# A hybrid decoder step on one core: the product of the squares' sum moved behind the third unit of the gated projection

## The chip, the core and the metric

One core of a Trainium2 chip runs the whole step as one program. The metric is the device time in microseconds of one execution; the time of a version is the median of its runs. The engines are TensorE (PE in the rows; its weight loads are PEld), VectorE (DVE), ScalarE (ACT), GpSimd (POOL) and SyncE (SP), which here issues most of the transfers.

## The reference

Two layers of a decoder run on 520 tokens (512 of a prompt and 8 new ones), with a width of 1024. Each layer normalizes its input, projects it once to 7424 columns, and feeds a convolution branch and an attention branch, which are gated, merged and added to the input. The parts that matter here:

```python
def rms_norm(x, g):
    xf = x.astype(jnp.float32)
    y = xf * lax.rsqrt(jnp.mean(xf * xf, axis=-1, keepdims=True) + EPS)
    return (y * g.astype(jnp.float32)).astype(x.dtype)

def hybrid_layer(x, ...):
    h = rms_norm(x, norm_g)
    z = jnp.einsum('ntd,dc->ntc', h, w_in)
    glu, gate_a, q, k, v, gate_b, mg_a, mg_b = split_in(z)
    u = glu[..., :CONV_WIDTH] * jax.nn.sigmoid(glu[..., CONV_WIDTH:])
    ...
    return x + jnp.einsum('ntd,de->nte', y, w_out), ...
```

## The kernel before, in words

**Layout.** Everything is held transposed: the width lies on the 128 partitions in 8 row tiles, and the 520 tokens on the free axis, in two halves of 260. All weights of a layer are cut into 82 blocks of 1024 x 128. One block is a `Unit` (line 101): it is loaded as `raw` (512 KB, line 123, by SP's queue), ScalarE casts it to a rounded `whi` (line 126), and VectorE makes the rest `wlo` (line 127). A row tile is likewise kept as a rounded part and a rest. `step(half, k)` (line 130) issues three matmuls: whi by the rounded row, wlo by the rounded row, whi by the row's rest. A half takes 8 steps, 24 matmuls, and a unit takes 48. There are two buffers of `raw` and three each of `whi` and `wlo`, so the load of a unit waits for the split (line 127) of the unit two before it, and its cast waits for the last matmul of the unit three before it.

**The start of a layer.** The gated projection takes 16 units, two for each of 8 column groups i: one for the sigmoid, one for the value. I number them from one: the first and second unit belong to i = 0, the third and fourth to i = 1, the fifth and sixth to i = 2, the seventh and eighth to i = 3, and the ninth begins i = 4. The first six units multiply the rows that are scaled by the norm's weight only (`xh`, `xl`), since the factor 1/rms is not known yet; it is multiplied in afterwards (lines 304 and 306). From the seventh on the units multiply the fully normed rows `hh` and their rests `hl`.

**The factor.** ScalarE squares the 8 row tiles (line 197), VectorE adds them up (line 165, seven additions to `ssum`). `totals` (line 175) multiplies the sum by a matrix of ones, one product for each half (line 170, in full float32; the trace shows each as two matmuls). `rstd` (line 178) takes the logarithm on ScalarE (L183), a scaled copy on VectorE (L184), the exponential on ScalarE (L186) and three more steps on VectorE (L187, L188, L189); its result is `R`. Then `normed` (line 263) makes the rows: L266 on VectorE multiplies by R, L97 on ScalarE casts, L98 on VectorE makes the rest. It is called for rows 0 to 2, 3 to 5 and 6 to 7, in the groups i = 0, 1 and 2. Its buffer `sq` has three places.

**The groups 0 to 2** copy the unit's results out of PSUM (lines 298 and 302, ScalarE), multiply by R (L304), take the sigmoid (L305), multiply by R again (L306) and by the value (L307). The result `u` goes to the convolution, which VectorE works off at low priority over the next hundreds of microseconds (L595).

**PSUM.** A unit's sums lie in one of two buffers `mm`. The third unit is `spare`: its halves lie in the tiles T and V instead, which are free at this stage, so that it can run before the first two units are copied out. A product of line 170 uses a tile S.

**What orders the work.** The text above does not fix the order on an engine. A planner runs through the program with its own idea of times and gives each engine, whenever it is free, the ready instruction that stands first in the text; the order that comes out is then fixed, and the engine keeps to it. `tc.issue_after(ins)` adds that what the block puts on the engine of `ins` is issued behind `ins`; it adds no wait for its end. `mark[1]` holds the last matmul issued (line 134). In the text of before, `R = rstd(sq.totals())` (line 286) stands behind the first two units and ahead of the third (line 289). In the first layer the first two units run as their rows arrive; in the second, they follow the previous layer's output.

Of the kernel before, what the change touches and what calls it, by code (L numbers as in the profile page):

```python
# [20 lines left out]
KT = 8  # L21
# [11 lines left out]
W_GLU, W_K, W_V, W_Q, W_GB, W_MB, W_MA, W_GA, W_YB, W_YA, W_OUT = (  # L33
    0, 16, 17, 18, 26, 34, 42, 50, 58, 66, 74)
# [10 lines left out]
def hybrid_step(ctx, tc, x_in, w_in, par, const, rope, conv_st, kc_in, vc_in,  # L45
# [17 lines left out]
    mark = [None, None, None]  # L63
# [5 lines left out]
    def g(dt=F32):  # L69
        return gp.tile([128, TOK], dt, tag="g", name=name("g"))  # L70
# [4 lines left out]
    def two(t):  # L75
        return t.rearrange("p (a b) -> p a b", a=2)
# [4 lines left out]
    def small(n):  # L81
        return sp.tile([128, n], F32, tag=f"sm{n}", name=name("sm"))

    def tmp(tag, bufs, n=TOK):
        return ap.tile([128, n], F32, tag=tag, bufs=bufs, name=name(tag))
# [9 lines left out]
    def split(src, n=TOK, new=g):  # L95
        hi, lo = new(F32R), new(F32R)
        A.copy(hi[:, :n], src)  # L97
        mark[0] = V.tensor_tensor(lo[:, :n], src, hi[:, :n].bitcast(F32), op=ALU.subtract)  # L98
        return hi, lo
# [78 lines left out]
    def rstd(sums, halves=(0, 1)):  # L178
        y0, v, a = tmp("y0", 1), tmp("v", 1), tmp("a", 1)
        c = slice(halves[0] * HALF, (halves[-1] + 1) * HALF)  # L180
        for hf, s in zip(halves, sums):
            h = slice(hf * HALF, (hf + 1) * HALF)
            A.activation(y0[:, h], s, AF.Ln, bias=eps, scale=1.0 / D)  # L183
            V.tensor_scalar(v[:, h], s, 1.0 / D, EPS, op0=ALU.mult, op1=ALU.add)  # L184
        y0, v, a = y0[:, c], v[:, c], a[:, c]
        A.activation(y0, y0, AF.Exp, scale=-0.5)  # L186
        V.scalar_tensor_tensor(a, y0, -0.5, y0, op0=ALU.mult, op1=ALU.mult)  # L187
        V.tensor_tensor(v, v, a, op=ALU.mult)  # L188
        V.scalar_tensor_tensor(v, v, 1.5, y0, op0=ALU.add, op1=ALU.mult)  # L189
        return v  # L190
# [33 lines left out]
    xs, xh, xl, sq = [], [], [], Sum()  # L224
# [28 lines left out]
    for l in range(L):  # L253
# [9 lines left out]
        def normed(lo, hi):  # L263
            for i in range(lo, hi):
                h = tmp("sq", 3)
                V.scalar_tensor_tensor(h, xs[i], pt[:, P_G + i:P_G + i + 1], R,  # L266
                                       op0=ALU.mult, op1=ALU.mult)
                a, b = split(h)
                hh.append(a)
                hl.append(b)  # L270
            return mark[0].ins

        EARLY = 3
        for i in range(KT):
            if i % 2 == 0:
                s = g()
                (nc.gpsimd if l else nc.sync).dma_start(s[:, :2 * NS * TAPS],
                                                        conv_st[l, :, i // 2, :])
                st.append(s[:, :2 * NS * TAPS].rearrange("p (i n k) -> p i n k", i=2, n=NS))
            src = (xh, xl) if i < EARLY else (hh, hl)  # L280
            if i == 0:
                for k in range(KT):
                    for u in first:
                        u.step(0, k)
                        u.step(1, k)
                R = rstd(sq.totals())
                a, b = first
            else:
                a = Unit(l, W_GLU + 2 * i, *src, spare=(i == 1))
                a.half(0)  # L290
                a.half(1)
            u = up.tile([128, PAD + TOK], F32, tag="u", name=f"u{l}_{i}")
            G.memset(u[:, :PAD], 0.0)
            uu = two(u[:, PAD:])
            sg = g()
            if i < EARLY:
                for hf in range(2):
                    A.copy(two(sg)[:, hf, :], a.acc[hf])
                if i > 0:
                    b = Unit(l, W_GLU + 2 * i + 1, *src)  # L300
                    b.both()
                A.copy(uu, b.ps)
                ready = normed((0, 3, 6)[i], (3, 6, 8)[i])
                V.tensor_tensor(sg, sg, R, op=ALU.mult)  # L304
                A.activation(sg, sg, AF.Sigmoid)  # L305
                V.tensor_tensor(sg, sg, R, op=ALU.mult)  # L306
                V.tensor_tensor(uu, uu, two(sg), op=ALU.mult)  # L307
            else:
                A.activation(two(sg), a.ps, AF.Sigmoid)
                z1 = Unit(l, W_GLU + 2 * i + 1, *src).both()  # L310
                V.tensor_tensor(uu, z1, two(sg), op=ALU.mult)
            V.tensor_copy(st[i // 2][:, i % 2, :, PAD:], u[:, PAD + T:].unsqueeze(2))
            nc.gpsimd.dma_start(ncp[l, :, i, :], u[:, T:T + PAD])
            us.append(u)
            if i % 2 == 1:
                nc.gpsimd.dma_start(ncs[l, :, i // 2, :],
                                    st[i // 2].rearrange("p i n k -> p (i n k)"))
                i0, pair = i - 1, (i - 1, i)
                n2 = 2 * NS * TAPS
                pr = tmp("sq", 3)[:, :n2]  # L320
                pr4 = pr.rearrange("p (i n k) -> p i n k", i=2, n=NS)
                wv = pt[:, P_CW + TAPS * i0:P_CW + TAPS * (i0 + 2)].rearrange("p (i k) -> p i k", i=2)
                for i in pair:
                    V.tensor_tensor(pr4[:, i - i0], st[i0 // 2][:, i - i0],
                                    wv[:, i - i0].unsqueeze(1).broadcast_to([128, NS, TAPS]),
                                    op=ALU.mult)
                sm = small(16)
                V.tensor_reduce(sm, pr.rearrange("p (m k) -> p m k", k=TAPS),
                                axis=mybir.AxisListType.X, op=ALU.add)
                for i in pair:  # L330
                    V.tensor_scalar(us[i][:, PAD + T:], sm[:, (i - i0) * NS:(i - i0 + 1) * NS],
                                    pt[:, P_CB + i:P_CB + i + 1], None, op0=ALU.add)
# [20 lines left out]
        for kv in range(2):  # L353
            a, b = g(F32R), g(F32R)
# [73 lines left out]
        for kv in range(2):  # L428
            src = qsam.rearrange("(t v) d n -> v d t n", v=2)[kv]
# [201 lines left out]
        for i in range(KT):  # L631
# [5 lines left out]
            a, b = split(e)  # L637
# [7 lines left out]
        for i in range(KT):  # L645
# [3 lines left out]
            a, b = split(mga[i], new=og)  # L649
# [14 lines left out]
        if not last:  # L664
            nres = dr.tile([128, KT, TOK], F32, tag="xres", bufs=1, name=f"xres{l}")
            pt = params(l + 1)
            xs, xh, xl, sq = [], [], [], Sum()
# [13 lines left out]
        sq = Sum()  # L681

        def finish(i, u, hf):
            x = two(xr[i])[:, hf, :]
            done = V.tensor_tensor(x, u.half(hf), x, op=ALU.add)  # L685
            s = tmp("sq", 3)
            A.activation(two(s)[:, hf, :], x, AF.Square)
            return sq.add(i, s, (hf,)) or done

        def scale(hf):  # L690
            return rstd([sq.total(hf)], (hf,))

        def store(hf, R, i0, i1):
            for i in range(i0, i1):
                x = two(xr[i])[:, hf, :]
                V.scalar_tensor_tensor(x, x, con[:, C_FG + i:C_FG + i + 1], R,  # L696
                                       op0=ALU.mult, op1=ALU.mult)
                (nc.sync if i % 2 else nc.scalar).dma_start(
                    y_out[:, i, hf * HALF:(hf + 1) * HALF], x)
# [10 lines left out]
        with tc.issue_after(mark[1].ins):  # L710
            R = scale(0)
            finish(5, units[0], 1)
# [117 lines left out]
```

## Time and profile before

| what | value |
|---|---|
| median of 3 runs | 1064.87 us |
| lowest and highest | 1064.74 and 1064.91 us |
| the profiled execution | 1064.98 us |
| its span, first to last instruction | 1063.2 us |
| mean granted clock of TensorE | 0.997 |
| instructions | 21526 |
| read from HBM, written to it | 107.66 MB, 17.36 MB |

The span is the time that the trace covers; the execution's own time has 1.78 us more around it. Times in rows are counted from the span's start. A row of the timeline gives the start, the time until the end of the last one, the engine, the line, the operation, the tile written and the tiles read, and how many instructions it merges. In brackets stands how long the engine was idle before it and what ended that.

### The profile page before, as it was taken

Reading aid. Unit: us, or ns where it says so; the run is one execution under the profiler, and the core shown is the slowest. Engines: PE = TensorE matmul, PEld = TensorE weight load, DVE = VectorE, ACT = ScalarE, POOL = GpSimd, SP = SyncE. Lnnn points to the kernel's source line nnn. Section 1 sums busy time; section 2 is a strip of 40 time slices with the busy share of each in tenths; the row PEclk is TensorE's granted clock in tenths of the full one; section 3 lists DMA queues with packets and bytes.
Section 4 is the critical chain, followed back from the end, with each engine's and each line's share of the span. In section 5 each row is a group of like instructions: output and inputs, shape, how many; then the busy total and the mean of one; then the engine's idle time right before and its main releaser. Section 6 shows DMA issues by size and latency. Waiting matters only on the chain.

```text
span 1063.2 us, 21526 instructions
## 1 busy us (share of the span) xinstructions
PE 1049.8 (99%) x8742; PEld 1034.9 (97%) x8742; DVE 855.4 (80%) x1572; ACT 516.5 (49%) x953; POOL 79.5 (7%) x180
## 2 busy tenths in 40 slices
PE   8999999999999999999999999999999999999996
PEld 8999999999999999999999999999999999999995
DVE  7999999999999587455569999899999976944545
ACT  7621433356667784224453234434576686822322
POOL 0001211001011000000101013100001000000000
PEclk9999999999999999999999999999999999999998
DMA  7334574332321215233334337633232212252312
GB/s 234 127 120 132 173 237 144 102 117 80 105 90 66 80 60 198 82 100 117 133 100 140 120 113 238 205 119 119 81 112 81 87 60 80 87 178 95 99 61 81
DMA packets 45220, 126.42 MB, mean 119 GB/s; under 512 B 6384, under 2 KB 10048, under 8 KB 45120
## 3 DMA queue, kind: packets, MB, share of 16 engines
q1 hardware_dynamic: 39024, 111.81, 32.0%
q0 software_dynamic: 4800, 12.16, 3.6%
q8 instruction: 68, 1.11, 0.4%
q10 hardware_dynamic: 1296, 1.07, 0.3%
q14 instruction: 32, 0.26, 0.1%
HBM read 107.66 MB, written 17.36 MB: 118 GB/s over the span
## 4 chain that ended last, share of the span: by engine, by line
PE 97%; DVE 1%; DMA 1%; SPq 0%; issue 0%; ACT 0%; DVEq 0%; ACTq 0%
PE mm L134 86%; PE S L506 3%; PE pv L541 3%; PE PT L532 2%; PE T L134 1%; PE S L170 1%; PE V L134 1%; DMA g<-x 1%; DMA raw<-w 0%; DVE g L696 0%; DVE ssum L165 0%; PE S L464 0%; PE pvs L486 0%; SPq L123 0%; PE S L348 0%
## 5 line engine op out<-in xcount | busy, mean ns | idle before, releaser
L134 PE MATMUL mm<-g,whi 128*128 128x260 f32 x4160 | 766.2, 284 | 1.0 <-ACT g L215 1.0
L134 PEld LDWEIGHTS mm<-g,whi 128*128 128x128 f32 x4160 | 644.8, 188 | 2.0 <-ACT g L215 1.2
L134 PE MATMUL mm<-g,wlo 128*128 128x260 f32 x2080 | 588.9, 283 | 0.0
L134 PEld LDWEIGHTS mm<-g,wlo 128*128 128x128 f32 x2080 | 392.0, 188 | 0.1
L595 DVE SCALAR_TENSOR_TENSOR acc<-u,par,acc 128x512 f32<-128x512 f32 x464 | 329.0, 744 | 0.2
L126 ACT CAST whi<-raw 128x1024 fp32r<-128x1024 f32 (+1 forms) x168 | 172.9, 1029 | 205.9 <-PE mm L134 165.1
L127 DVE TENSOR_TENSOR wlo<-raw,whi 128x1024 fp32r<-128x1024 f32 (+1 forms) x168 | 200.8, 1196 | 52.7 <-ACT whi L126 52.4
L134 PE MATMUL mm<-o,whi 128*128 128x260 f32 x992 | 179.3, 282 | 1.0 <-DVE g L685 1.0
L134 PEld LDWEIGHTS mm<-o,whi 128*128 128x128 f32 x992 | 153.1, 188 | 1.5 <-issue 0.8
L134 PE MATMUL mm<-o,wlo 128*128 128x260 f32 x496 | 139.5, 282 | 0.0
L134 PEld LDWEIGHTS mm<-o,wlo 128*128 128x128 f32 x496 | 93.2, 188 | 0.0
L518 ACT ACTIVATE p<-p,sm 128x257 f32<-128x257 f32 (+1 forms) x128 | 60.9, 479 | 18.7 <-DVE sm L512 18.6
L512 DVE CUSTOM_DVE_ANT_0 p<-S,con,nsk 128x256 f32<-128x256 f32 (+1 forms) x128 | 52.8, 447 | 7.9 <-PE PT L532 6.1
L534 ACT COPY pts<-PT 128x256 f32<-128x256 f32 (+1 forms) x64 | 33.7, 526 | 50.2 <-PE PT L532 50.2
L510 POOL COPY p<-nsk 128x2 f32<-128x2 f32 x64 | 26.0, 413 | 342.9 <-PE PT L532 289.0
L647 DVE TENSOR_TENSOR g<-mm,g 128x520 f32<-128x520 f32 x16 | 11.2, 700 | 43.1 <-PE mm L134 43.1
L506 PE MATMUL S<-g,g 128*128 128x256 f32 x256 | 41.6, 283 | 0.0
L445 ACT ACTIVATE g<-mm 128x520 f32<-128x520 f32 x16 | 9.7, 606 | 56.7 <-PE mm L134 56.7
L532 PE MATMUL PT<-con,p 128*128 128x128 f32 x224 | 35.6, 276 | 0.0
L506 PEld LDWEIGHTS S<-g,g 128*128 128x128 f32 x256 | 35.1, 188 | 0.0
L641 DVE TENSOR_TENSOR g<-mm,g 128x520 f32<-128x520 f32 x16 | 11.1, 695 | 28.8 <-PE mm L134 28.8
L522 ACT ACTIVATE p<-p,sm 128x128 f32<-128x128 f32 (+1 forms) x64 | 30.5, 480 | 7.5 <-DVE sm L521 7.3
(168 smaller groups left out, 817.5 us busy)
## 6 DMA issues: line engine op xcount, KB each, us to landing
raw<-w SPq DMA_DIRECT2D x162, 512.0 KB, 3.4
qscr<-g SPq DMA_DIRECT2D x32, 256.0 KB, 4.3
g<-qscr SPq DMA_DIRECT2D x32, 256.0 KB, 3.8
g<-x SPq DMA_DIRECT2D x16, 260.0 KB, 4.9
g<-rope POOLq DMA_DIRECT2D x8, 260.0 KB, 4.6
xres<-g POOLq DMA_DIRECT2D x8, 260.0 KB, 2.3
g<-xres SPq DMA_DIRECT2D x8, 260.0 KB, 4.9
ncs<-g POOLq DMA_DIRECT2D x8, 248.0 KB, 3.1
```

Source lines behind the costliest of these rows:

```text
L126: mark[2] = A.copy(self.hi[:, ks, :], self.raw[:, ks, :])
L127: mark[0] = V.tensor_tensor(self.lo[:, ks, :], self.raw[:, ks, :], self.hi[:, ks, :].bitcast(F32), op=ALU.subtract)
L134: mark[1] = PE.matmul(self.acc[hf], a[:, k, :], b[k][:, c], start=(k == 0 and j == 0), stop=(k == KT - 1 and j == 2))
L506: PE.matmul(S3[:, kv, :], qs[t, kv][:, b * 128:b * 128 + 128], K[kv][:, k0:k0 + 256], start=(j == 0), stop=(j == 1))
L510: G.tensor_copy(p[:, :, nk:nk + 1], nsk[:, 2 * t:2 * t + 2].unsqueeze(2))
L512: V.tensor_tensor_reduce(out=p[:, kv, :nk], in0=S3[:, kv, :nk], in1=con[:, C_MASK + 256 - nk:C_MASK + 256], op0=ALU.add, op1=ALU.min, scal ...
L518: exp_ins[0] = A.activation(p[:, kv, :nk + 1], p[:, kv, :nk + 1], AF.Exp, bias=nm[:, kv:kv + 1], scale=-1.0, accum_out=dn[:, kv:kv + 1])
L522: A.mul(p[:, 0, :nk], p[:, 0, :nk], dn[:, 0:1])
L532: PE.transpose(PT[:, kv, kb, :], p[:, kv, kb * 128:kb * 128 + 128], ident)
L534: A.copy(pts[t][:, :, j0:j0 + nb, :], PT[:, :, :nb, :])
L541: PE.matmul(pv[kv * 64:kv * 64 + 64, j * 128:(j + nb) * 128], vb[:, j * 128 + kv * 64:j * 128 + kv * 64 + 64], pts[t][:, kv, 2 * j:2 * j + ...
L595: V.scalar_tensor_tensor(dst, us[i][:, k:k + T], cw(i, k), acc[i], op0=ALU.mult, op1=ALU.add)
```

## The change

In every layer the third unit is now built, and its 48 matmuls are written, ahead of the product of the squares' sum: its first half, then the eight steps of its second half, of which the last matmul of step k = 2, the ninth of that half, is kept as `far`. Then come the products, in the first layer under a tie behind `far`, in the second without a tie, and then `rstd`. The group i = 1 takes the unit that was built so, and no other unit is `spare`.

```diff
                     for u in first:
                         u.step(0, k)
                         u.step(1, k)
-                R = rstd(sq.totals())
+                second = Unit(l, W_GLU + 2, *src, spare=True)
+                second.half(0)
+                for k in range(KT):
+                    second.step(1, k)
+                    if k == 2:
+                        far = mark[1]
+                if l == 0:
+                    with tc.issue_after(far.ins):
+                        sums = sq.totals()
+                else:
+                    sums = sq.totals()
+                R = rstd(sums)
                 a, b = first
+            elif i == 1:
+                a = second
             else:
-                a = Unit(l, W_GLU + 2 * i, *src, spare=(i == 1))
+                a = Unit(l, W_GLU + 2 * i, *src)
                 a.half(0)
                 a.half(1)
```

## Rows read from the trace of the kernel before

**Rows 1.** The page: busy time, share of the span and instructions by engine.
```profile
PE 1049.8 (99%) x8742; PEld 1034.9 (97%) x8742; DVE 855.4 (80%) x1572; ACT 516.5 (49%) x953; POOL 79.5 (7%) x180
```
**Rows 2.** The page: the chain that ended last, by engine.
```profile
PE 97%; DVE 1%; DMA 1%; SPq 0%; issue 0%; ACT 0%; DVEq 0%; ACTq 0%
```
**Rows 3.** Waits of TensorE: who waited for whom, us in total, times, longest.
```profile
PE S L170 <- DVE ssum L165: 1.3, 1, 1.3
```
**Rows 4.** Timeline of the first layer around the product: TensorE, then VectorE and ScalarE.
```profile
20.62 0.28 PE L134 MATMUL T<-g,wlo 128*128 128x260 f32 x1
...
22.20 1.14 PE L170 MATMUL S<-ssum,ones 128*128 128x260 f32 x4 [1.29 <-DVE ssum L165]
...
18.23 3.91 DVE L165 TENSOR_TENSOR ssum<-ssum,sq 128x520 f32<-128x520 f32 x5
22.06 2.52 DVE L127 TENSOR_TENSOR wlo<-raw,whi 128x1024 fp32r<-128x1024 f32 x2
24.50 0.76 DVE L184 TENSOR_SCALAR v<-S 128x260 f32<-128x260 f32 x2
25.17 0.69 DVE L187 SCALAR_TENSOR_TENSOR a<-y 128x520 f32<-128x520 f32 x1
...
26.63 0.70 DVE L189 SCALAR_TENSOR_TENSOR v<-v,y 128x520 f32<-128x520 f32 x1
...
23.20 0.87 ACT L183 ACTIVATE y<-S,eps 128x260 f32<-128x260 f32 x2
24.10 0.64 ACT L186 ACTIVATE y<-y 128x520 f32<-128x520 f32 x1
26.70 1.05 ACT L126 CAST whi<-raw 128x1024 fp32r<-128x1024 f32 x1 [1.96 <-PE V L134]
```
**Rows 5.** Two stretches: us, then busy time of PE, PEld, DVE, ACT, POOL; PEclk, DMA, GB/s.
```profile
26.50:43.70 17.20, 17.20 (x147) 17.20 (x146) 17.13 (x27) 13.25 (x20) 1.26 (x2) 1.00 0.33 104
...
547.50:565.00 17.50, 17.50 (x148) 17.50 (x147) 17.50 (x28) 12.56 (x21) 1.62 (x3) 1.00 0.35 103
```
**Rows 6.** Timeline of the first layer at the seventh and eighth units: VectorE, then TensorE.
```profile
45.45 1.23 DVE L127 TENSOR_TENSOR wlo<-raw,whi 128x1024 fp32r<-128x1024 f32 x1 [0.20 <-ACT whi L126]
...
47.53 0.69 DVE L307 TENSOR_TENSOR u<-u,g 128x520 f32<-128x520 f32 x1
48.15 0.69 DVE L98 TENSOR_TENSOR g<-sq,g 128x520 fp32r<-128x520 f32 x1
...
48.24 0.28 PE L134 MATMUL mm<-g,whi 128*128 128x260 f32 x1
...
49.20 0.41 PE L134 MATMUL mm<-g,whi 128*128 128x260 f32 x2
```
**Rows 7.** Timeline of the second layer at the like places: TensorE, ScalarE, VectorE, TensorE.
```profile
540.88 1.04 PE L170 MATMUL S<-ssum,ones 128*128 128x260 f32 x4
...
547.40 0.28 PE L134 MATMUL V<-g,whi 128*128 128x260 f32 x1
...
547.72 1.05 ACT L126 CAST whi<-raw 128x1024 fp32r<-128x1024 f32 x1 [2.91 <-PE V L134]
...
546.70 0.70 DVE L189 SCALAR_TENSOR_TENSOR v<-v,y 128x520 f32<-128x520 f32 x1
...
566.57 1.23 DVE L127 TENSOR_TENSOR wlo<-raw,whi 128x1024 fp32r<-128x1024 f32 x1 [1.25 <-ACT whi L126]
...
569.26 0.69 DVE L98 TENSOR_TENSOR g<-sq,g 128x520 fp32r<-128x520 f32 x1
...
570.32 0.40 PE L134 MATMUL mm<-g,whi 128*128 128x260 f32 x2
```
**Rows 8.** Timeline: the rotary product (line 348) and the copy that it needs.
```profile
106.95 0.59 ACT L339 COPY g<-mm 128x520 f32<-128x520 f32 x1 [4.67 <-PE mm L134]
...
112.48 1.04 PE L348 MATMUL S<-g,con 128*128 128x260 f32 x4
```
**Rows 9.** The page: transfers of weight blocks, KB each, us from issue to landing.
```profile
raw<-w SPq DMA_DIRECT2D x162, 512.0 KB, 3.4
```

## The prediction, made before the change was run

> **What bounds the kernel now.** I began with the page's busy times: TensorE is busy for 99% of the span, VectorE for 80% [rows 1]. The chain of work that ended last says the same, 97% of it TensorE [rows 2]. So a microsecond taken from or added to TensorE's idle time shows in full in the result, and one anywhere else shows only if it makes TensorE wait. TensorE's waits are few: five in all, and the longest is the one that the change is about, 1.3 us of the product of the squares' sum (line 170) for the sum itself [rows 3]. 1.3 us is 0.12% of the run; a measurement of this kernel can tell about 0.2% (2.13 us) from no change. If everything goes as meant, the result still counts as no change. The question is whether something costs more than that.
>
> I then read that place in order of time [rows 4]. TensorE runs the third unit's first half (tile T) until its matmul at 20.62, then nothing until 22.20: the five additions of the sum hold VectorE from 18.23 to 22.14. The product starts at 22.20, and the rest of T and the second half (tile V) follow it. Beside the wait, VectorE is the engine to look at: in the 17.20 us after it VectorE is busy 17.13, and in the like 17.50 us of the second layer 17.50 [rows 5]. TensorE is full there too, at a granted clock of 1.00 (the level of 2.4 GHz). In this stage both engines are full, and a wait removed on one is worth only what the other can follow.
>
> **Who waits for whom behind it.** The product feeds ScalarE's logarithms (L183) and VectorE's rstd (L184 to L189), ready at 27.33 in the first layer. On rstd hang the normed rows, which the seventh and eighth units multiply. TensorE takes those two units in turns, because the last two rows are late: the one lone whi at 48.24 breaks the pattern of two and one. The last rest is made by L98 from 48.15 to 48.84, and its first reader on TensorE, by the kernel's own order, starts at 49.20 [rows 6]. So the slack there is 0.36 us, and the only idle time of VectorE in front of it 0.20. In the second layer the same places read 569.26 + 0.69 = 569.95 against 570.32, slack 0.37, with 1.25 us of idle VectorE in front [rows 7].
>
> **The change, part by part.** The same instructions are issued, no DMA more or less: two products (each in two passes), the third unit's 48 matmuls, its load and its split all remain. What changes is the text order, and the planner gives an engine the ready instruction that stands first in the text. The tie keeps the product behind the ninth matmul of V; it does not pull it there. The other 15 matmuls of V now stand ahead of the product in the text and are ready. The trace has a like case: the rotary product of line 348 needs the copy of line 339, which ends at 107.54, yet it starts at 112.48, right after all 48 matmuls of the unit that stands between them in the text [rows 8]. So I expect the product behind V's last matmul, and **in both layers**, since the text is moved in both and only the tie is limited to the first.
>
> First layer. T goes on at 20.74 instead of standing until 22.20. Its last 4 and V's 24 matmuls, at 0.12 us each (eight lie between 48.24 and 49.20 in the rows below), take 3.36 us, and the product starts at 24.1, 1.9 later than before. At this point TensorE has gained the idle 1.29 us. The product takes 1.14, so the logarithms (0.87 the two) end near 25.24 + 0.44 = 25.7 and L186 (0.64) near 26.35. L187 then starts at 26.4 instead of 25.17: rstd is 1.2 us later [rows 4]. Before, the split of the fifth unit's weights held VectorE until 24.58, which hid part of the delay. The last rest comes 1.2 - 0.20 - 0.36 = 0.65 us later than its reader started before. L307 (0.61 net, 47.53) stands between the last two rests and feeds no product [rows 6]; it stands later in the text and went first only because its neighbour was not ready, which a late VectorE changes. Between 0.65 and 0.04 I take **+0.1**: the gain of 1.29 is all given back at the seventh and eighth units. Bounds: the split of the ninth unit's weights (1.23) also goes behind, -1.1; or see the third rival, +2.5.
>
> Second layer. There is no wait to remove: the product starts at 540.88, V's last matmul at 547.40 [rows 7]. Behind 48 matmuls of 0.12 the product starts near 546.6, and its 1.04 us end near 547.65. ScalarE's cast of the sixth unit's weights, which V's end releases (547.72 now), becomes ready first and takes 1.05 from 546.9; the logarithms (0.87) end at 548.8, L186 at 549.45. VectorE splits those weights meanwhile (1.23, until 549.2), then L184 (0.76), L187, L188 and L189 at 0.73 each: rstd at 552.0 instead of 547.40, 4.6 us later. The split no longer stands in the chain behind rstd (1.14 net), which leaves 3.4. Idle time covers 1.25 of it and the slack 0.37: TensorE waits 1.8 us with L307 in place, 1.2 without. I take **+1.4**, nearer to the lower. Bounds: 0 if the ninth unit's split goes behind as well, 2.3 if the cast falls between the two logarithms (some 0.5 more than 1.8). TensorE's other stages stay as they are: what is queued on SP and POOL (weight loads, small stores) is released 1 to 4 us later at most, while the casts and splits run units ahead.
>
> The sum is 1064.98 (the profiled execution; its span is 1063.2, with 1.78 around it) + 0.1 + 1.4 = 1066.48. That run stands 0.11 over the median of 1064.87, so against the median I say **1066.4**, 0.14% slower, which is no change by the bound above.
>
> A rule to weigh: VectorE, full on both sides of the gap [rows 5], isn't given less to do. The Trainium skill, "Perfetto Trace Analysis", section "Identifying Performance Opportunities" (Optimization Strategy), says to find the gaps of the engine one optimizes and to make what they wait for start sooner or finish faster. It speaks against this change, which fills the gap and leaves what it waited for as it is. By that advice alone nothing is won here and nothing lost, 1064.98; by the rows above the first layer gives the same, and the second adds its 1.4.
>
> **Rivals.**
> *The tie places the product.* It runs behind V's ninth matmul, and in the second layer where it was. Then it starts at 22.3, the sum (22.14) is just ready, and rstd does not move, since L184 at 24.50 waits for the split's end. TensorE is ahead by 1.3 until the last rest, which can come 0.20 sooner; 0.20 + 0.36 = 0.56 is won: 1064.3. For it: the ninth matmul is just where the wait would end. Against it: rows 8. Chance 0.13.
> *The gap is closed and stays closed*, if VectorE's order also drops work from in front of the last rests: 1064.87 - 1.3 = 1063.6. Against it: 17.13 of 17.20. Chance 0.05.
> *Slower: the sixth unit's cast goes ahead of the logarithms in the first layer too.* Its weights can load only once the fourth unit's split ends (22.06 + 1.23 = 23.3), and with 3.4 us to land [rows 9] they are there at 26.7, when the cast starts now [rows 4]. If the planner thinks them landed sooner, ScalarE stands at that cast, the logarithms start at 27.75, and rstd comes at 31.5, 4.2 late. Less 1.14 for the split, 0.20 and 0.36 that is +2.5 instead of +0.1: 1068.8. It decides when the order on ScalarE has the cast before either logarithm. Chance 0.20.
>
> **How the numbers follow.** My forecast has 0.62; its own range is 1065.0 (+0.1 and nothing lost in the second layer) to 1067.8 (+0.65 and +2.3). To hold the time 8 times in 10 the range takes in the first rival at 1064.3 and most of the third: 1064.2 to 1068.9. Slower than 1067.0 are nearly all of the third rival (0.18) and the upper part of the forecast (0.16): 0.34. Faster than 1062.74 is no case here, 0.02 for what I overlook. The rest, 0.64, is no change.
>
> **What would show it.** In the changed profile: no wait of line 170 for the sum; the product behind 24 matmuls of V in both layers; the last L189 near 28.5 and 552; new waits of TensorE for L98 (or its cast L97) near 49 and 570, some 1.4 us each, in place of the one of 1.3. I am wrong if the product stands among V's matmuls, or if TensorE does not wait at the seventh and eighth units though rstd is later.

## The result, and the profile after

The changed kernel takes 1073.08 us in the median of 6 runs (1071.87 to 1073.95), the kernel before 1064.84 beside it: 8.2 us slower, ratio 1.0076, 95% interval 1.0063 to 1.0089. The forecast was 1066.4, its range ended at 1068.9. The profiled execution took 1073.19, its span 1071.4.

The page of the changed kernel, the busy times and the first line of the chain, to hold against [rows 1, 2]:

```profile
PE 1053.9 (98%) x8742; PEld 1038.1 (97%) x8742; DVE 855.6 (80%) x1572; ACT 518.9 (48%) x955; POOL 75.1 (7%) x180
...
PE 89%; DVE 6%; ACT 2%; DMA 1%; issue 1%; SPq 0%; DVEq 0%; ACTq 0%
```

TensorE has the same 8742 matmuls, but is busy 4.1 us longer, and a tenth of the chain is now other engines. ScalarE has two instructions more. The waits of TensorE in the changed kernel, as in [rows 3]:

```profile
PE mm L134 <- ACT g L97: 2.6, 1, 2.6
PE mm L134 <- DVE g L98: 2.3, 2, 1.7
...
PE mm L134 <- ACT g L311: 1.0, 1, 1.0
```

The wait of line 170 is gone, as the forecast said. In its place stand four others: 1.01, 1.69, 0.64 and 2.60 us, 5.94 together. Why TensorE is busier shows in its clock. Stretches of the changed kernel, columns as in [rows 5] (PEclk is the third number from the end):

```profile
51.60:55.00 3.40, 3.40 (x19) 3.40 (x19) 3.40 (x8) 0.00 (x0) 0.54 (x1) 0.55 0.17 66
55.00:58.00 3.00, 3.00 (x28) 3.00 (x27) 3.00 (x7) 1.54 (x2) 0.00 (x0) 1.00 0.00 0
...
932.20:935.60 3.40, 3.40 (x19) 3.40 (x18) 3.40 (x6) 3.35 (x5) 0.00 (x0) 0.54 0.50 154
```

Right behind the wait of 1.69 and right behind that of 2.60 the granted clock is at its lower level (0.5, 1.2 GHz) for about 3.4 us, and 19 matmuls go through where 28 do in 3.00 us at 1.00. Each such stretch costs half its length, 1.7 us. The sum: 5.94 idle; 0.16 more at each of the four waits (the last matmul before a wait shows 0.28, while the next would have started 0.12 behind it); 3.4 for the clock; less the 1.45 of the old wait, counted alike. That is 8.5 against the 8.2 measured. The start does not explain the 0.3: the wait for the first rows is 0.40 here and 1.04 before, but the matmuls near 10 us start within 0.15 us of the same ones before. What is left lies in smaller steps that were not followed.

**First layer.** The changed kernel around the product, as [rows 4]: TensorE, ScalarE, VectorE.

```profile
23.64 0.28 PE L134 MATMUL V<-g,whi 128*128 128x260 f32 x1
23.76 1.04 PE L170 MATMUL S<-ssum,ones 128*128 128x260 f32 x4
...
21.94 1.07 ACT L126 CAST whi<-raw 128x1024 fp32r<-128x1024 f32 x1
26.39 1.05 ACT L126 CAST whi<-raw 128x1024 fp32r<-128x1024 f32 x1 [3.38 <-DMA raw<-w]
27.35 0.83 ACT L183 ACTIVATE y<-S,eps 128x260 f32<-128x260 f32 x2
28.21 0.64 ACT L186 ACTIVATE y<-y 128x520 f32<-128x520 f32 x1
...
27.47 1.23 DVE L127 TENSOR_TENSOR wlo<-raw,whi 128x1024 fp32r<-128x1024 f32 x1 [3.21 <-ACT whi L126]
...
30.75 0.70 DVE L189 SCALAR_TENSOR_TENSOR v<-v,y 128x520 f32<-128x520 f32 x1
```

The product is done at 24.80. ScalarE stands until 26.39, not for it but for a transfer: the cast of the sixth unit's weights is now ahead of the logarithms in its order, and those weights have not landed. The logarithms start at 27.35, and rstd is ready at 31.45 instead of 27.33. What follows, at the places of [rows 6]: ScalarE, TensorE; VectorE, TensorE.

```profile
41.77 0.61 ACT L97 CAST g<-sq 128x520 fp32r<-128x520 f32 x1
42.28 0.64 ACT L311 COPY g<-mm 128x260 f32<-128x260 f32 x2
...
42.97 0.39 PE L134 MATMUL mm<-g,whi 128*128 128x260 f32 x1 [1.01 <-ACT g L311]
...
49.29 0.69 DVE L98 TENSOR_TENSOR g<-sq,g 128x520 fp32r<-128x520 f32 x1
...
50.03 0.51 PE L134 MATMUL mm<-g,whi 128*128 128x260 f32 x2 [1.69 <-DVE g L98]
```

First a copy out of PSUM (L311, L298 before) waits on ScalarE behind a late cast of a normed row, and TensorE lacks the accumulators that it frees. Then the last two rests come at 49.98 and 50.92, where the last came at 48.84; TensorE goes on with the first of them.

**Second layer.** The places of [rows 7]: the cast (released by V, as before, but ahead of the logarithms), rstd, and the reader of the last rests.

```profile
549.73 1.05 ACT L126 CAST whi<-raw 128x1024 fp32r<-128x1024 f32 x1 [3.48 <-PE V L134]
...
554.09 0.70 DVE L189 SCALAR_TENSOR_TENSOR v<-v,y 128x520 f32<-128x520 f32 x1
...
573.37 0.51 PE L134 MATMUL mm<-g,whi 128*128 128x260 f32 x2 [0.64 <-DVE g L98]
```

**A third place, 360 us further on.** It lies in the second layer's second normalisation (that of the convolution's output), whose text the change does not touch. Before, in order of time:

```profile
904.61 1.04 PE L170 MATMUL S<-ssum,ones 128*128 128x260 f32 x4
...
906.61 0.85 ACT L183 ACTIVATE y<-S,eps 128x260 f32<-128x260 f32 x2
907.48 1.28 ACT L186 ACT_TABLE_LOAD   x1
908.77 0.64 ACT L186 ACTIVATE y<-y 128x520 f32<-128x520 f32 x1
...
912.01 0.69 DVE L189 SCALAR_TENSOR_TENSOR v<-v,y 128x520 f32<-128x520 f32 x1
```

And in the changed kernel:

```profile
908.70 1.04 PE L170 MATMUL S<-ssum,ones 128*128 128x260 f32 x4
...
910.26 0.48 ACT L183 ACTIVATE y<-S,eps 128x260 f32<-128x260 f32 x1
910.76 1.28 ACT L639 ACT_TABLE_LOAD   x1
912.05 0.64 ACT L639 ACTIVATE sq<-g 128x520 f32<-128x520 f32 x1
912.71 1.28 ACT L183 ACT_TABLE_LOAD   x1
914.00 0.48 ACT L183 ACTIVATE y<-S,eps 128x260 f32<-128x260 f32 x1
914.38 0.59 ACT L633 COPY g<-mm 128x520 f32<-128x520 f32 x1
914.85 1.06 ACT L126 CAST whi<-raw 128x1024 fp32r<-128x1024 f32 x1
...
917.22 0.64 ACT L186 ACTIVATE y<-y 128x520 f32<-128x520 f32 x1
...
921.19 0.70 DVE L189 SCALAR_TENSOR_TENSOR v<-v,y 128x520 f32<-128x520 f32 x1
...
930.62 0.36 PE L134 MATMUL mm<-o,whi 128*128 128x260 f32 x1 [2.60 <-ACT g L97]
```

The planner has put a gate unit's sigmoid (L639) between the two logarithms. The functions use different tables, so ScalarE loads twice more, 1.28 each; a copy and a cast that ran behind the Exp now run ahead of it. From the product's start to the end of L189 it was 8.09 us, now it is 13.19: 5.1 later, and TensorE stands 2.60.

### The profile page after: what moved, and what is told of

The parts are those of the page before. It is cut to its first block, busy times and chain, and to the rows that moved or that the text cites. A ratio compares the mean times of both kernels' runs of the same rounds, so it can differ in the third digit from the quotient of the medians.

```text
span 1071.4 us, 21531 instructions
## 1 busy us (share of the span) xinstructions
PE 1053.9 (98%) x8742; PEld 1038.1 (97%) x8742; DVE 855.6 (80%) x1572; ACT 518.9 (48%) x955; POOL 75.1 (7%) x180
## 4 chain that ended last, share of the span: by engine, by line
PE 89%; DVE 6%; ACT 2%; DMA 1%; issue 1%; SPq 0%; DVEq 0%; ACTq 0%
PE mm L134 79%; PE S L519 3%; PE pv L554 2%; PE PT L545 2%; DVE wlo L127 1%; DVE sq L266 1%; DVE g L98 1%; DMA raw<-w 1%; PE T L134 1%; DMA g<-x 0%; ACT whi L126 0%; DVE g L709 0%; DVE u L626 0%; PE S L477 0%; PE pvs L499 0%
## 5 line engine op out<-in xcount | busy, mean ns | idle before, releaser
L523 POOL COPY p<-nsk 128x2 f32<-128x2 f32 x64 | 21.4, 341 | 346.1 <-PE PT L545 252.2
```

The lines of the kernel that those rows point to most:

```text
L523: G.tensor_copy(p[:, :, nk:nk + 1], nsk[:, 2 * t:2 * t + 2].unsqueeze(2))
```

## The experiments

The question was how much of the 8.2 belongs to each of the three places, and what makes the wait at each. Lines of kernels that add lines are a few higher; the text says which.

**Without the tie.**

```
-                if l == 0:
-                    with tc.issue_after(far.ins):
-                        sums = sq.totals()
-                else:
-                    sums = sq.totals()
+                sums = sq.totals()
```

> The changed kernel without its tie: in both layers the product stands behind the unit's 48 matmuls in the text and is tied to nothing. If the text's place alone decides (as the forecast had it), all is as in the changed kernel: product behind 24 matmuls of V, waits of 1.0, 1.7, 0.6 and 2.6, 21 table loads, 1072 to 1074. If the tie has a part in it (first rival), the product moves and the time falls to 1064 to 1069.

1072.89 (ratio 1.0075, 1.0058 to 1.0092). On every engine the order is the changed kernel's, row for row: the tie does nothing, the place in the text does all. Its profile has the same waits, and one thing more to see:

```profile
50.70:52.40 1.70, 1.69 (x12) 1.53 (x13) 1.70 (x4) 0.00 (x0) 0.00 (x0) 1.00 1.00 364
52.40:55.80 3.40, 3.40 (x30) 3.40 (x30) 3.40 (x9) 0.87 (x2) 0.54 (x1) 1.00 0.15 55
929.90:933.30 3.40, 3.40 (x17) 3.40 (x17) 3.40 (x6) 1.93 (x3) 0.00 (x0) 0.50 0.46 135
```

Behind the same waits of 1.01 and 1.69 the clock holds in this execution; behind the 2.60 it falls again. So the 1.7 us of the first layer come in some executions and not in others.

**One layer alone.** The new text order in the first layer only:

```
+                if l:
+                    sums = sq.totals()
                 second = Unit(l, W_GLU + 2, *src, spare=True)
...
                 if l == 0:
                     with tc.issue_after(far.ins):
                         sums = sq.totals()
-                else:
-                    sums = sq.totals()
```

> The new text order in the first layer alone; in the second the product stands ahead of the unit again, as before. Theory A (three separate places: two waits of 1.01 and 1.69 with 1.7 of half clock in layer 1, 0.64 in layer 2, and 2.60 with 1.7 of half clock near 930 that comes only from two more table loads between the logarithms of the second normalisation): the second layer's two places are gone here, its ScalarE has the two logarithms side by side, so before + 2.8 = 1067.6, with TensorE's waits near 43 and 50 as in the changed kernel and none after 540. Rival B (the stall near 930 is a late echo of the first layer, for example of transfers that are out of step): it stays, 1072.

1067.21 beside 1064.98 (ratio 1.002, 1.001 to 1.0029): +2.2. TensorE waits 1.04 at 43.52 and 1.69 at 50.58, and behind 540 only where the kernel before waits too. The ten executions lie half at 1066.1 to 1066.8 and half at 1067.6 to 1068.2, 1.6 apart, which is the price of one half-clock stretch; the profiled one (1068.04) has it. So the layer costs about 1.4 without that stretch and 3.0 with it, and 2.2 is a median between two groups.

In the second layer only, the mirror of that edit:

> The new text order in the second layer alone; the first layer as before, with its gap of 1.3 us at the product. Theory A: the 0.64 of layer 2 and no more, since here too the two logarithms of the second normalisation stand side by side: 1065.5, at most 1066. Rival B (the stall near 930 hangs on the second layer's late product): before + 0.6 + 4.3 = 1069.7.

1066.42 (ratio 1.0013, 1.0003 to 1.0022): +1.4. One new wait, 0.78 at 570.35, with 0.12 more behind it for the very last rest. With the beats lost around the two, TensorE falls back 1.2 there: so much later, against the same matmuls before, start those at 575 than those at 560. Both kernels load tables 19 times, and neither has a wait near 930. So rival B falls in both, and of these three the third place appears only where both layers have the new order: 8.2 - 2.2 - 1.4 leaves 4.6 for it, where each of the three is known to about 1 us.

**The cast behind the Exp.** The changed kernel, and the sixth unit's cast tied behind rstd's Exp in both layers (`rstd.exp` is that Exp):

```
-            mark[2] = A.copy(self.hi[:, ks, :], self.raw[:, ks, :])
+            with (tc.issue_after(held.pop()) if held else nullcontext()):
+                mark[2] = A.copy(self.hi[:, ks, :], self.raw[:, ks, :])
...
+                behind = rstd.exp
...
+                    if i == 2 and True:
+                        held.append(behind)
                     b = Unit(l, W_GLU + 2 * i + 1, *src)
```

> The changed kernel, with the cast of the sixth unit's weights held behind the Exp of rstd in both layers; on TensorE the order of all instructions is as in the changed kernel, and the table loads near 910 stay. Theory A (the cast ahead of the logarithms makes rstd 4 us late and so the waits of layers 1 and 2): rstd comes near 28.3 instead of 31.45, the 1.01 + 1.69 + 1.7 of half clock shrink to at most 0.7, the 0.64 of layer 2 goes: 1068 to 1069, the 4.3 near 930 left. Rival C (the product's own place, 24 matmuls later, is what costs, and ScalarE's order does not matter): 1072 to 1073.

1071.32 (ratio 1.0058, 1.0043 to 1.0073): 1.8 less than the changed kernel, where 4 to 5 were expected and rival C gave 0 to 1. The waits of 1.01 and 1.69 become one of 1.25, and the clock holds behind it; but the second layer's 0.64 becomes 1.20. VectorE tells why, here in the first layer (this kernel's L190 and L191 are L188 and L189, its L129 the split):

```profile
26.98 0.70 DVE L190 TENSOR_TENSOR v<-v,a 128x520 f32<-128x520 f32 x1
27.70 1.23 DVE L129 TENSOR_TENSOR wlo<-raw,whi 128x1024 fp32r<-128x1024 f32 x1
28.84 0.69 DVE L191 SCALAR_TENSOR_TENSOR v<-v,y 128x520 f32<-128x520 f32 x1
```

The logarithms are early, but the sixth unit's split goes between the last two steps of rstd: 29.53, 1.9 sooner than in the changed kernel and 1.0 later than the forecast had it. In the second layer the split goes there too, and nothing is won: from the product's start to rstd it takes 5.44 us, against 5.26 in the changed kernel. The cast matters, in the first layer and for less than theory A said, since the split behind it stands in the same chain either way.

**The sigmoids behind the Exp.** The changed kernel, the last three gate units' sigmoids of the second layer tied:

```
+        exp2 = rstd.exp
...
-                A.activation(sg, s, AF.Sigmoid)
+                with (tc.issue_after(exp2) if last and i >= 5 else nullcontext()):
+                    A.activation(sg, s, AF.Sigmoid)
```

> The changed kernel, with the sigmoids of the last three gate units of the second layer held behind the Exp of the second normalisation, so that its two logarithms stand side by side and ScalarE loads its tables 19 times instead of 21; the cast of the sixth unit is left where the change put it. Theory A: the wait of 2.60 near 930 and its 1.7 of half clock go: 1073.1 - 4.3 = 1068.8. Rival D (the wait near 930 is made by VectorE's queue, not by the table loads): 1072 to 1073.

1068.18 (ratio 1.0029, 1.0016 to 1.0041): 4.9 less, 4.3 expected. No wait near 930, no half clock there; the waits of both layers (0.54, 1.70 and 0.63) and the half clock behind the 1.70 are left. So more than half of the loss hangs on where the planner put the sigmoids.

**Both.** The two edits together:

> The changed kernel with both the cast of the sixth unit held behind the Exp of rstd in both layers and the last three gate units' sigmoids held behind the Exp of the second normalisation: ScalarE in the order that the forecast had assumed, TensorE in the order of the changed kernel. Theory A (the places add up): 1071.3 for the cast alone, less the 4.9 that the sigmoids alone gave back: 1066.4, with waits of about 1.25 near 48 and 1.2 near 570, none near 930, and no stretch of half clock before the tail. Rival E (the two places share their loss): 1068 or more.

1067.03 (ratio 1.0021, 1.0012 to 1.003), 0.6 over theory A: waits of 1.25 and 1.21, no half clock before the tail. Rival E falls, the places add up to within that 0.6.

**The table loads alone**, put into the kernel before:

```
-            A.activation(y0[:, h], s, AF.Ln, bias=eps, scale=1.0 / D)
+            with (tc.issue_after(between.ins) if more and hf else nullcontext()):
+                log = A.activation(y0[:, h], s, AF.Ln, bias=eps, scale=1.0 / D)
+            if more and not hf:
+                with tc.issue_after(log.ins):
+                    between = A.activation(small(1), eps, AF.Sigmoid)
...
-        R2 = rstd(sm.totals())
+        R2 = rstd(sm.totals(), more=last)
```

> The kernel before, with one sigmoid of 128x1 elements put between the two logarithms of the second layer's second normalisation, so that ScalarE loads its tables twice more there; nothing else in the order of any engine differs, and the output is the same. Theory A: 2 loads of 1.28 and the small sigmoid make that normalisation some 2.8 us late or more, TensorE waits near 924 and falls to half clock behind it: 1064.98 + 3 to 4.5 = 1068 to 1069.5. Rival D (the table loads lie beside TensorE's work and cost nothing; the wait near 930 came from another part of the new order): 1065.0.

1065.81 (ratio 1.001, 1.0001 to 1.0019): +1.0, a miss of theory A. ScalarE and TensorE:

```profile
906.30 0.48 ACT L184 ACTIVATE y<-S,eps 128x260 f32<-128x260 f32 x1
906.79 1.28 ACT L187 ACT_TABLE_LOAD   x1
908.09 0.20 ACT L187 ACTIVATE sm<-eps 128x1 f32<-128x1 f32 x1
908.31 1.28 ACT L184 ACT_TABLE_LOAD   x1
909.61 0.48 ACT L184 ACTIVATE y<-S,eps 128x260 f32<-128x260 f32 x1
...
924.76 0.36 PE L134 MATMUL mm<-o,whi 128*128 128x260 f32 x1 [0.46 <-ACT g L97]
```

The end of rstd (L189 in the other kernels) comes 2.94 us later against its product, and at this wait TensorE loses 0.46 + 0.16 = 0.62; the other 2.3 are slack. A shorter pause at 912.57, behind a gate unit's copy that is late too, and small steps add 0.3, which makes the 0.9 to 1.0 of the time. With that slack, 5.1 late makes 2.8 lost, and the changed kernel lost 2.60 + 0.16 = 2.76; that is one pair of numbers, set side by side after both were known. The loads are half of the 5.1; the rest is the sigmoid, the copy and the cast ahead of the Exp, and on VectorE L188, which stands behind the product with the next sigmoid (1.25 us idle for it). The Trainium skill, "ScalarE: Activation LUTs", section "What ACT_TABLE_LOAD costs", gives a load of about 1283 ns and with a drain 2.66 us for a change of table. The rows agree with the first (1.28) and show no second: a load starts 0.01 to 0.02 after the activation before it, and the next activation 0.01 to 0.02 after the load.

Four loads instead of two (logarithm and sigmoid once more):

> The kernel before, with three activations of 128x1 elements (sigmoid, logarithm, sigmoid) between the two logarithms of the second layer's second normalisation, so that ScalarE loads its tables four times more there. Theory A with a slack (two loads made the scale of that normalisation 2.94 us later against its product, and TensorE lost 0.62; in the changed kernel it was 5.1 later, and 2.76 were lost; so 2.3 are slack and the rest is lost): 5.8 later here, 3.5 lost, and half clock behind it: 1064.8 + 3.5 = 1068.3 where the clock holds, 1070 where it falls. Rival D (the wait of the changed kernel came from VectorE's order or from the transfers there): less than 1.0 lost, 1066.

1069.05 (ratio 1.0038, 1.0024 to 1.0052), in the expected range, with one wait and then the lower clock:

```profile
915.40 0.58 PE L134 MATMUL mm<-o,whi 128*128 128x260 f32 x1 [2.94 <-ACT g L627]
```

The stretch behind it:

```profile
915.40:918.70 3.30, 3.30 (x15) 3.30 (x16) 3.15 (x5) 3.27 (x5) 0.00 (x0) 0.50 0.07 16
```

But it is another wait: at 915 TensorE lacks accumulators that a gate unit's copy frees, and the copy stands behind the parted logarithms. The size came out and the mechanism did not. It shows that ScalarE's queue there stops TensorE by two ways, and it is no second proof of the 2.3.

**What the tie was to do.** In the first layer the product in the text among V's matmuls, in the second as before:

```
+                if l:
+                    sums = sq.totals()
                 second = Unit(l, W_GLU + 2, *src, spare=True)
...
                     second.step(1, k)
-                    if k == 2:
-                        far = mark[1]
-                if l == 0:
-                    with tc.issue_after(far.ins):
+                    if k == 2 and l == 0:
                         sums = sq.totals()
-                else:
-                    sums = sq.totals()
```

> What the tie was to do: in the first layer the product stands in the text among V's matmuls, behind the ninth; in the second layer ahead of the unit as before. The gap at 20.9 closes and rstd should not move. Theory F (VectorE's slack before the last rests decides): 0.56 won of the 1.3, 1064.4, and no wait of TensorE near 48. Rival G (the gap stays closed): 1063.7. Rival H (the gain is given back in full near 48): 1065.0.

1066.83 (ratio 1.0018, 1.0009 to 1.0027), over all three theories. In its profile the start took 1.8 more (a wait of 1.29 for the first rows, and half clock behind it). A second profile:

> product_in_v once more, for a second profile. If the 2.0 us that it lost against before come from the start (in its first profile TensorE stood 1.29 for the first rows and ran at half clock from 7.8 to 11.2), the start is the same again, and behind it TensorE's matmuls run 1.4 ahead of before up to 80 us. If the start is chance, the wait for the first rows is between 0.3 and 1.0 as in the other profiles, and a time of 1066 to 1067 has to show another place.

1067.06 (ratio 1.0019, 1.001 to 1.0028). The start is chance: 0.71 this time. Then:

```profile
48.80 0.51 PE L134 MATMUL mm<-g,whi 128*128 128x260 f32 x2 [1.53 <-DVE g L98]
```

The gap is closed, and TensorE waits at the last rests instead, for more than it won: the gain is given back near 48, as rival H has it. But rstd did move. VectorE around its last steps, in the second profile:

```profile
26.06 0.70 DVE L188 TENSOR_TENSOR v<-v,a 128x520 f32<-128x520 f32 x1
28.05 1.23 DVE L127 TENSOR_TENSOR wlo<-raw,whi 128x1024 fp32r<-128x1024 f32 x1 [1.29 <-ACT whi L126]
29.20 0.69 DVE L189 SCALAR_TENSOR_TENSOR v<-v,y 128x520 f32<-128x520 f32 x1
```

The product starts at 22.46, near its 22.20 before. But the planner has put the sixth unit's split ahead of rstd's last step; VectorE stands 1.29 for the cast that the split needs, and rstd is ready at 29.89 instead of 27.33. So this run does not show what the closed gap is worth with rstd as early as before. That VectorE decides at 48 the first profile bears out: its product starts 1.45 later (23.91), its rstd is ready at 29.67 all the same, and TensorE, late from the start, reaches the last rests without a listed wait. Of the rest of the 2.0 the largest step, 0.7, lies near 354, where TensorE's order is another one and it waits 0.40 for a copy (L544); the others are smaller and were not followed.

The same, and the ninth unit's split tied behind the last rests in the first layer:

> As product_in_v, and in the first layer VectorE's split of the ninth unit's weights (1.14 net) held behind the last rests of the normed rows. Theory F: the last rests come about 0.5 sooner still, the gap is closed and stays closed: 1064.98 - 1.3 = 1063.7. Rival H (the place near 48 is not what holds the gain back): the same time as product_in_v within 0.2.

1069.36 (ratio 1.0039, 1.0027 to 1.0052). The wait at 48 shrinks to 0.23, but the planner now parts the two logarithms of the first layer's second normalisation, and TensorE stands there:

```profile
405.20 0.36 PE L136 MATMUL mm<-o,whi 128*128 128x260 f32 x1 [2.58 <-ACT g L98]
```

It is the third place once more, in another layer, from another edit, with nearly the same wait. But behind this one the clock holds: it is 1.00 from 405.20 to 408.60. The profiled execution took 1067.93; of the five, two lie at 1067.9 and three at 1069.4 to 1070.3. The sigmoids tied there as well (in both layers):

> As product_in_v_split_behind (product among V's matmuls in the first layer, ninth unit's split behind the last rests), and the last three gate units' sigmoids held behind the Exp of the second normalisation in both layers, so that no two logarithms are parted: 19 table loads. Theory A: the wait of 2.6 that the profile of product_in_v_split_behind has at 403 goes with its half clock, 1069.4 - 4 = 1065 or less; with the gap of 1.3 closed and nothing else moved, 1063.7. Rival E (the loss at 403 is not the table loads): 1068 to 1069.

1065.67 (ratio 1.0006, 0.9996 to 1.0015): the wait near 405 (the expectation's 403) is gone, 3.7 less. 0.65 and 0.23 stand near 48, rstd is late here too (29.81, VectorE stands 1.55 for the same split), and what the gap gave is used up by the end. This version cannot be told from the kernel before, and none here beats it.

## Why the prediction was wrong, point by point

- **The product's place: right.** It runs behind V's 24 matmuls in both layers, and without the tie every engine has the same order.
- **Second layer, +1.4: right.** The layer alone costs 1.4. The cast ahead of the logarithms and rstd 4.6 later, at 552.0, were the forecast's; alone, L189 ends at 551.76. Only the single wait was put too long, at some 1.4: it is 0.78 in the layer alone and 0.64 in the changed kernel, and TensorE falls back 1.2 with what is lost around it.
- **First layer, +0.1: wrong, the third rival took its place.** It had 0.20: cast ahead of the logarithms, rstd at 31.5 (31.45 measured), +2.5. The layer alone shows 2.2, but that nearness is luck: it is 1.4 where the clock holds and 3.0 where it falls, and the rival had no clock. The failing step is that the cast's place on ScalarE was taken over from before. Where it is held back, the wait of 1.25 (1.41 with the beat) uses up the 1.45 of the gap, so the +0.1 came out with the order that it assumed. Its rstd at 28.5 did not (29.53, the split in between).
- **Missing from every case: the clock.** Each wait was priced at its length. Behind the 1.01 and 1.69, and behind the 2.60, TensorE ran at 1.2 GHz for about 3.4 us, 1.7 us more each (the first in some executions only); behind the single waits of 1.29 [rows 3], 1.25 and 1.20 it did not. The forecast put this term at nothing; it is 3.4 of the 8.2 in the profiled execution.
- **"TensorE's other stages stay as they are": wrong, and the largest error.** The third place costs 4.6, as what the two layers alone leave over, and 4.9 by taking it away. The argument looked at what would be released later on the chip. But the planner orders the whole kernel anew: compared place by place, 900 of VectorE's 1572 instructions and 183 of ScalarE's 934 (table loads left out) are others than before, the last of them at 936 and 931 us. In both layers' new order it parted two logarithms 360 us downstream. Without it the kernel takes 1068.18. That this is near the third rival's 1068.8 is in part luck: the rival has longer waits in the first layer than were measured, and half clock, which it does not have, fills the difference. With both edits, ScalarE in the forecast's order, it takes 2.2 more than before, where the forecast had 1.5. Why the planner parts them with both layers changed, and not with one of these two changes alone, stays open.
- **The rule weighed: not settled.** The rule would have it that filling a gap wins nothing while what it waited for is left as it is. No run here tests that cleanly. In product_in_v the 1.3 came back as 1.53 at the last rests, but there rstd was also 2.6 late, by the split ahead of its last step. The first rival, whose order on TensorE this is in the first layer, had priced it at 0.56 won, with rstd unmoved; 2.0 were lost.

## What to carry to other kernels

Where a planner orders the engines, an edit of the text is an edit of every later stage: compare the order on each engine, the table loads of ScalarE first (19 and 21 here), before arguing about the place edited. Tie functions that share a table together where a scale waits for them. And close a gap of a full engine only after asking who must be sooner at the next meeting point: in every run here that closed it, rstd came later and a wait stood there or elsewhere instead, and two waits close together cost the clock as well in some executions.

## What the runs showed of the hardware

TensorE's clock fell behind short waits within an otherwise full stretch, to 0.5 for about 3.4 us each time. Behind one wait of 2.58 to 2.94 it fell in four profiles (the changed kernel, no_tie, cast_behind, four_more_loads) and held in one (2.58 in product_in_v_split_behind). Behind two waits 7 us apart, the second of 1.69 or 1.70, it fell in three (the changed kernel, first_layer_only, sigmoid_behind) and held in no_tie, which has the changed kernel's order. Behind single waits of 1.20 to 1.53 in a full stretch it held; behind 1.29 at the start of product_in_v, when TensorE had only begun, it fell. So the length of the wait alone does not decide. The Trainium skill, "TensorE: Matmul & The Clock Gate", section "What's actually happening", says that what the gate watches runs on its own and does not start anew with a kernel, so that the point where the clock changes varies between runs. The two profiles with the same order, one with the fall and one without, fit that and do not show the reason.
